# Alternating high and low products, with a short filler matmul, in the second part of each column tile of two input projections

## The chip, the cores and the metric

The kernel runs on one core of a Trainium2 chip. The metric is the device time of one execution in microseconds; the time of a kernel is the median of its runs.

## What is computed

The reference is a two-layer decoder trunk over 256 tokens of width 1024 in float32. Each layer is a half-step SwiGLU block (2816 hidden columns), a mixer, and a second half-step SwiGLU block. Layer 0 mixes with a short gated convolution, layer 1 with a sparse attention that reads keys and values made once between the layers. What the change touches is the second SwiGLU block of both layers:

```python
def swiglu_ffn(x, w_in, w_out):
    gate, up = jnp.split(x @ w_in, 2, axis=-1)
    return (jax.nn.silu(gate) * up) @ w_out
...
    h = h + 0.5 * swiglu_ffn(rmsnorm(h, ffn2_norm[i]), ffn2_w_in[i], ffn2_w_out[i])
```

Here `x @ w_in` is the input projection: 256 x 1024 by 1024 x 5632.

## The kernel before

**Split products.** Activations lie transposed, 128 features by 256 tokens in each of eight tiles. A float32 value is split into a high part, rounded to the operand type float32r, and a low part, the remainder in the same type. An activation tile `xs[k]` is 128 x 512: 256 columns of high parts, then 256 of low parts. A weight block of 128 x 128 has a high version `wh` (`u[0]`) and a low version `wl` (`u[1]`). One product of a block is then two matmuls: the *high product*, `wh` against all 512 columns of `xs[k]` (line 331), and the *low product*, `wl` against the 256 high columns (line 333). Both add into one PSUM bank; the two halves of the bank are added later. The next text calls one high and one low product a pair. Each matmul loads its own weights.

**Column tiles.** `ffn_in` makes an input projection. For each of 22 column tiles f it takes a double bank (`bank2`, tile `mm`, two of them in rotation) and fills two parts, the gate columns and the up columns, each by eight pairs (one for each k). `a_group` takes two weight units from the stream and calls `a_pass` for each part. `a_pass` issues the pairs in runs: `run` high products, then the `run` low products of the same k. `RUNS` sets a run of 2 for all tiles. In tile 0 both parts stop before k = 7, and a callback `mid` makes the row sums of the norm (`norm.rows`, which takes a bank from the pool `a` of four banks); after that come the last pairs. After a tile `total`, `times` and `ffn_evac` on ScalarE and VectorE make the hidden columns (lines 342 to 359).

**Weights.** `Stream` brings the weights by DMA from SyncE. Units of 128 x 1024 are split by ScalarE (high, line 150) and VectorE (low, line 167), up to `NBUF` = 6 units ahead. `weave` puts these conversions between the steps of an evacuation. A tile gives its two units back after its last matmul (`W.done`).

**Order.** The kernel is scheduled by hand: each engine runs its instructions in program order. The two projections that the change touches stand between two output projections (`out_proj`, lines 440 and 442, in runs of 2 too) or, in layer 1, behind the attention.

**Other places named below.** `b_full` (lines 550 to 552) and lines 821 to 823 are projections whose matmuls are all of 512 columns. Line 453 is a series of 256-column products at the end, line 656 one in the compression. Line 628 transposes 128 x 128 blocks; line 667 is two fp32 products of 64 columns; line 305 the fp32 product of the norm's row sums, 256 columns.

Of the kernel before, what the change touches and what calls it, by code (L numbers as in the profile page):

```python
# [9 lines left out]
F32 = mybir.dt.float32  # L10
# [6 lines left out]
P = 128  # L17
T = 256
# [15 lines left out]
LAG = 4  # L34
NBUF = 6
CHUNK = 2048
EXP4 = (0, 1, 2, 3, 4, 5)
ORDER = """
    q00.0 q00.1 q00.2 norm_pe q00.3 norm_act:A norm_dve:D q01.0 qsq00:A qsum00:D q01.1 uh6:A qsqrt00:A ul6:D q01.2 uh7:A qrec00:D ul7:D qrr00:P q01.3
# [22 lines left out]
def trunk(ctx, tc, A, out):  # L62
    nc = tc.nc
    ve, ac, pe, po, sy = nc.vector, nc.scalar, nc.tensor, nc.gpsimd, nc.sync
# [9 lines left out]
    def mk(shape, tag, bufs, dt=F32, pool=None):  # L74
        uid[0] += 1
        return (pool or sb).tile(list(shape), dt, tag=tag, name=f"{tag}_{uid[0]}", bufs=bufs)
# [4 lines left out]
    def bank(shape=(P, 512)):  # L81
        return mk(shape, "a", 4, pool=ps)

    def bank2():
        return mk([P, 2, 512], "mm", 2, pool=ps)
# [14 lines left out]
    class Stream:  # L100
# [7 lines left out]
        def add(self, src, lo=0, hi=None, joint=0):  # L108


            hi = src.shape[1] if hi is None else hi
            while lo < hi:
                n = min(CHUNK, hi - lo)
                for u in range(max(n // 1024, 1)):
                    self.where.append((len(self.src), u, joint))
                self.src.append(src[:, lo:lo + n])
                lo += n

        def load(self, c):
            while self.loaded <= min(c, len(self.src) - 1):  # L120
                st = mk([P, CHUNK], "ws", 3)
                src = self.src[self.loaded]
# [66 lines left out]
    W = Stream()  # L189
# [32 lines left out]
    h = [hall[:, c] for c in range(ND)]  # L222
    first = [mk([P, CHUNK], "ws", 3) for _ in range(2)]
    for q in range(6):
# [12 lines left out]
    ident = small[:, S_ID:S_ID + P]  # L237
# [6 lines left out]
    def tables():  # L244

        sy.dma_start(small, A["small"])
        po.memset(rb, NEG)
        sy.dma_start(rb[:NB], A["rel_bias"])
        oh = t2()
        sy.dma_start(oh[:NB + 1], A["onehot"])  # L250
        yield
        pr = bank()
        pe.matmul(pr[:16], rb, oh[:NB + 1], start=True, stop=True)
        row = t2()
        ac.activation(row[:16], pr[:16], AF.Copy, scale=-1.0)
        sy.dma_start(row_d, row[:16])


    def new_xs():
        return [mk([P, 512], "xs", 8, F32R) for _ in range(8)]  # L260
# [62 lines left out]

    RUNS = (2, 2, 2, 2)

    def a_pass(o, u, xs, ks, last=7, run=2):

        ks = list(ks)
        for i in range(0, len(ks), run):
            for k in ks[i:i + run]:  # L330
                pe.matmul(o, u[0][:, k * P:(k + 1) * P], xs[k], start=(k == 0), stop=False)  # L331
            for k in ks[i:i + run]:
                pe.matmul(o[:, :T], u[1][:, k * P:(k + 1) * P], xs[k][:, :T], start=False, stop=(k == last))  # L333
# [5 lines left out]
    def total(o, n):  # L339

        r = t2([P, n, T])
        ac.copy(r, o[:, :, T:])  # L342
        ve.tensor_tensor(out=r, in0=o[:, :, :T], in1=r, op=ALU.add)  # L343
        return r
# [4 lines left out]
    def weave(gen):  # L349
        for _ in gen:  # L350
            W.pump(1)
        W.pump()

    def ffn_evac(r, R, hid):
        times(r, R, 2)
        yield
        s = t1()
        ac.activation(s, r[:, 0], AF.Silu)  # L358
        ve.tensor_tensor(out=s, in0=s, in1=r[:, 1], op=ALU.mult)  # L359
        yield  # L360
        hd = act()
        split(s, hd)
        hid.append(hd)

    def a_group(parts, xs, mid=None, run=2):
        us = W.take(len(parts))
        if mid is None:
            for o, u in zip(parts, us):
                a_pass(o, u, xs, range(8), run=run)
        else:  # L370
            for o, u in zip(parts, us):
                a_pass(o, u, xs, range(7))
            mid()
            for o, u in zip(parts, us):
                a_pass(o, u, xs, [7])
        W.done(len(parts), False)

    def ffn_in(xs, norm, R=None, bg=None, pre=None, late=False):
        hid, sums = [], []
        box = [R]  # L380

        def mid():
            if pre is not None:
                pre()
            box[0] = norm.rows()

        for f in range(NF):
            o = bank2()
            if late and f < 2:

                u = W.take(2)
                a_pass(o[:, 0], u[0], xs, range(8))
                if f == 1:
                    W.pump(1)
                    mid()
                a_pass(o[:, 1], u[1], xs, range(8))
                W.done(2, False)
            else:
                a_group([o[:, 0], o[:, 1]], xs, mid if f == 0 and R is None else None, RUNS[f % 4])
            sums.append(total(o, 2))  # L400
            while len(sums) > (1 if late and f < LAG else 0):
                weave(ffn_evac(sums.pop(0), box[0], hid))
            if bg is not None:
                bg(f)
        return hid
# [57 lines left out]
    xs = new_xs()  # L463
    nm = Norm([(xs, G_FFN1)])
# [14 lines left out]
    half(1, 1)  # L479
    W.pump(2)  # L480
    hid = ffn_in(xs, nm, late=True)
    xs = new_xs()
    nm = Norm([(xs, G_MIX)])
# [39 lines left out]
    xs = new_xs()  # L523
    nm = Norm([(xs, G_FFN2)])
    tab = tables()
    next(tab)
    out_proj(zs, 1.0, nm)
    hid = ffn_in(xs, nm, pre=lambda: list(tab))


    xs = new_xs()
# [3 lines left out]
    nm = Norm([(xkv, G_KV), (xs, G_FFN1 + 8)])  # L535
# [172 lines left out]
    def bg(f):  # L708

        if f == 0:  # L710
            kv["s"] = squares(kns)
        elif f == 1:
            r = inv_rms(kv["s"])
            for tt in range(2):
                v = kns[tt].rearrange("p (n d) -> p n d", d=64)
                po.tensor_tensor(out=v, in0=v, in1=r[:, tt * 8:tt * 8 + 8, None].to_broadcast([P, 8, 64]), op=ALU.mult)
        elif f in (2, 3, 4, 5):
            c_trans((f - 2) % 2, (f - 2) // 2)
        elif f in (6, 7):
            k_trans(f - 6)  # L720
        elif f == 8:
            po.tensor_tensor(out=both, in0=ident[:, :64], in1=ident[:, 64:], op=ALU.add)
            po.tensor_tensor(out=both48, in0=ident[:96, :48], in1=ident[:96, 48:96], op=ALU.add)
        elif f == 9:
            kv["rk"] = rh_split(0)
        elif f == W1AT[0]:
            kv["ak"] = c_hidden(kv["rk"])
        elif f == 12:
            kv["ak"] = c_total(kv["ak"])
            kv["rv"] = rh_split(1)  # L730
            W.limit = NBUF
        elif f == W1AT[1]:
            kv["av"] = c_hidden(kv["rv"])
            kv["kc"] = kc_norm(c_second(kv["ak"], 0))
        elif f == 15:
            kv["av"] = c_total(kv["av"])
        elif f == 16:
            kc_trans(kv["kc"])
        elif f == 17:
            pc = c_second(kv["av"], 1)  # L740
            for q in range(4):
                ac.copy(vc[32 * q:32 * q + 15, q % 2].rearrange("p (b a d) -> p b a d", a=2, d=64)[:, :, q // 2],
                        pc[:15, :256].rearrange("p (b a d) -> p b a d", a=2, d=64)[:, :, q // 2])

    hid = ffn_in(xs, None, R1, bg)
    xs = new_xs()
    nm = Norm([(xs, G_MIX + 8)])
# [227 lines left out]
    def pair_ops(p):  # L975
# [138 lines left out]
        add(f"M0{p}", m0)  # L1114
        if p in EXP4:
            add(f"U0{p}", e0s)
# [115 lines left out]
    xs, nm = xs2, nm2  # L1232
    W.at = u0 + 9 + ND
    W.pump()
    del oT
    hid = ffn_in(xs, nm)
    class Store:
        def tile(self, c):
            sy.dma_start(out[c], h[c])
# [69 lines left out]
```

## Time and profile before

| | us |
|---|---|
| median of 3 runs | 988.7 |
| lowest, highest | 988.3, 990.07 |
| the profiled execution, its own time | 990.75 |
| span of the profiled execution | 988.9 |

The profile is of one execution. PE stands for TensorE's matmuls, PEld for its weight loads, DVE for VectorE, ACT for ScalarE, POOL for GpSimd, SP for SyncE; "mm<-xs,wl" means that the tile mm is written from xs and wl. In the timeline each row is a start in us, a duration, the engine and line, the operation, and how many such instructions follow each other; an instruction's end is modelled, and matmuls overlap in the records, so the distance of two starts is the cost of a step. In the rows of stretches, (x...) is the number of instructions, PEclk the granted share of TensorE's clock. The two projections in question run from about 288.0 to 412.2 us (layer 0) and from 801.0 to 924.0 us (layer 1); tiles 1 to 21 of them begin at 295.18 and 806.99 us.

### The profile page before, as it was taken

The numbers are of one execution on the slowest core, as the hardware profiler recorded it, in microseconds if no ns is written. First come the engines' busy times: TensorE is split into PE (matmuls) and PEld (weight loads), VectorE is DVE, ScalarE is ACT, GpSimd is POOL, SyncE is SP. The second block draws the span as 40 slices with busy tenths as digits, with TensorE's granted clock in tenths as the row PEclk, the third lists the DMA queues.
The fourth block names the chain that finished last, engine by engine and source line by source line (L and its number), as shares of the span: only waits on it lengthen the run. The fifth ranks groups of instructions, "written<-read, shape, count | busy, mean of one in ns | idle before, by whom it ended". The sixth has DMA issues, their size and how long they took to land.

```text
span 988.9 us, 14575 instructions
## 1 busy us (share of the span) xinstructions
PE 976.5 (99%) x5672; PEld 838.3 (85%) x5672; DVE 745.8 (75%) x1078; ACT 560.3 (57%) x905; POOL 163.8 (17%) x235
## 2 busy tenths in 40 slices
PE   8999999999999999999999999999989999999998
PEld 6888888888888888888888888888867788888887
DVE  7887876568888787867549988866589788787752
ACT  4765654445556565644556677644469466655530
POOL 5000001144460000011011022011256420000000
PEclk8999999999999999999999999999999999999999
DMA  7655555545546555565544566654810455655550
GB/s 236 240 207 176 206 203 181 179 151 197 205 141 245 176 204 174 198 204 195 174 140 155 203 223 213 209 203 149 229 71 1 133 173 206 199 185 187 202 186 22
DMA packets 28720, 177.58 MB, mean 180 GB/s; under 512 B 3259, under 2 KB 6587, under 8 KB 7916
## 3 DMA queue, kind: packets, MB, share of 16 engines
q1 hardware_dynamic: 28652, 176.66, 52.6%
q8 instruction: 44, 0.72, 0.3%
q14 instruction: 24, 0.20, 0.1%
HBM read 175.57 MB, written 1.08 MB: 179 GB/s over the span
## 4 chain that ended last, share of the span: by engine, by line
PE 96%; DVE 2%; POOL 1%; issue 0%; DMA 0%; ACT 0%; SPq 0%; POOLq 0%; DVEq 0%; ACTq 0%
PE mm L331 37%; PE mm L333 18%; PE a L440 17%; PE a L442 8%; PE a L331 3%; PE a L333 1%; PE a L550 1%; PE a L552 1%; PE a L551 1%; PE a L1065 1%; PE a L821 1%; PE mm L999 1%; PE a L1081 1%; PE a L822 1%; PE a L823 1%; PE mm L990 0%
## 5 line engine op out<-in xcount | busy, mean ns | idle before, releaser
L331 PE MATMUL mm<-xs,wh 128*128 128x512 f32 x1536 | 488.5, 399 | 2.7 <-DVE xs L281 2.2
L167 DVE TENSOR_TENSOR wl<-ws,wh 128x1024 fp32r<-128x1024 f32 x322 | 400.4, 1247 | 82.9 <-ACT wh L150 82.5
L150 ACT CAST wh<-ws 128x1024 fp32r<-128x1024 f32 x322 | 335.8, 1046 | 89.6 <-PE a L440 58.5
L333 PEld LDWEIGHTS mm<-xs,wl 128*128 128x128 f32 x1536 | 289.6, 189 | 69.1 <-DVE wl L470 0.8
L333 PE MATMUL mm<-xs,wl 128*128 128x256 f32 x1536 | 304.2, 279 | 0.5 <-DVE wl L470 0.5
L331 PEld LDWEIGHTS mm<-xs,wh 128*128 128x128 f32 x1536 | 235.8, 189 | 5.7 <-DVE xs L281 4.3
L440 PE MATMUL a<-act,wh 128*128 128x512 f32 x722 | 226.7, 395 | 0.0
L442 PEld LDWEIGHTS a<-act,wl 128*128 128x128 f32 x722 | 135.6, 188 | 32.1
L442 PE MATMUL a<-act,wl 128*128 128x256 f32 x722 | 141.8, 278 | 0.0
L343 DVE TENSOR_TENSOR t<-mm,t 128x512 f32<-128x512 f32 x96 | 66.1, 689 | 76.4 <-ACT t L342 75.7
L342 ACT COPY t<-mm 128x512 f32<-128x512 f32 x96 | 56.1, 585 | 103.6 <-PE mm L333 103.5
L440 PEld LDWEIGHTS a<-act,wh 128*128 128x128 f32 x722 | 109.9, 189 | 0.0
L358 ACT ACTIVATE t<-t 128x256 f32<-128x256 f32 x88 | 36.8, 419 | 63.7 <-DVE t L347 63.6
L347 DVE TENSOR_TENSOR t<-t,R 128x512 f32<-128x512 f32 x88 | 61.6, 700 | 2.8
L336 ACT CAST act<-t 128x256 fp32r<-128x256 f32 x96 | 39.0, 407 | 28.1 <-DVE t L504 19.1
L287 POOL TENSOR_TENSOR sq<-hall 128x256 f32<-128x256 f32 x5 | 3.1, 615 | 295.9 <-DVE hall L409 294.1
L290 POOL TENSOR_TENSOR t<-hall 128x256 f32<-128x256 f32 x35 | 27.4, 783 | 134.8 <-DVE hall L409 134.6
L280 ACT ACTIVATE xs<-hall,gains 128x256 fp32r<-128x256 f32 x40 | 19.7, 504 | 50.6 <-DVE hall L409 47.5
L337 DVE TENSOR_TENSOR act<-t,act 128x256 fp32r<-128x256 f32 x96 | 40.9, 426 | 4.3 <-ACT act L336 4.3
L409 DVE SCALAR_TENSOR_TENSOR hall<-a,hall 128x256 f32<-128x256 f32 x78 | 32.9, 422 | 14.4 <-PE a L442 12.1
L359 DVE TENSOR_TENSOR t<-t,t 128x256 f32<-128x256 f32 x88 | 36.9, 419 | 4.0 <-ACT t L358 4.0
L281 DVE SCALAR_TENSOR_TENSOR xs<-hall,gains,xs 128x256 fp32r<-128x256 f32 x40 | 27.5, 696 | 15.1 <-ACT xs L280 15.1
(238 smaller groups left out, 810.2 us busy)
## 6 DMA issues: line engine op xcount, KB each, us to landing
ws<-in_ffn_w_in_dram SPq DMA_DIRECT2D x86, 1024.0 KB, 4.9
ws<-in_ffn_w_out_dram SPq DMA_DIRECT2D x44, 1024.0 KB, 4.8
ws<-in_conv_w_in_dram SPq DMA_DIRECT2D x12, 1024.0 KB, 4.8
ws<-in_w_kv_dram SPq DMA_DIRECT2D x6, 1024.0 KB, 4.8
ws<-in_conv_w_out_dram SPq DMA_DIRECT2D x4, 1024.0 KB, 4.8
ws<-in_attn_w_q_dram SPq DMA_DIRECT2D x4, 1024.0 KB, 4.9
ws<-in_attn_w_o_dram SPq DMA_DIRECT2D x4, 1024.0 KB, 9.1
act<-row_d SPq DMA_DIRECT2D x8, 256.0 KB, 9.1
```

The costliest lines, as they stand in the source:

```text
L150: ac.copy(h, src)
L167: e.tensor_tensor(out=l, in0=src, in1=h.bitcast(F32), op=ALU.subtract)
L331: pe.matmul(o, u[0][:, k * P:(k + 1) * P], xs[k], start=(k == 0), stop=False)
L333: pe.matmul(o[:, :T], u[1][:, k * P:(k + 1) * P], xs[k][:, :T], start=False, stop=(k == last))
L336: ac.copy(dst[:, :T], src)
L337: ve.tensor_tensor(out=dst[:, T:], in0=src, in1=dst[:, :T].bitcast(F32), op=ALU.subtract)
L342: ac.copy(r, o[:, :, T:])
L343: ve.tensor_tensor(out=r, in0=o[:, :, :T], in1=r, op=ALU.add)
L347: ve.tensor_tensor(out=r, in0=r, in1=R[:, None, :].to_broadcast([P, n, T]), op=ALU.mult)
L359: ve.tensor_tensor(out=s, in0=s, in1=r[:, 1], op=ALU.mult)
L440: pe.matmul(o, wh, lhs[k], start=(k == 0), stop=False)
L442: pe.matmul(o[:, :T], wl, lhs[k][:, :T], start=False, stop=(k == n - 1))
```

## The change

`ffn_in` gets a table `mixed`, one entry (first, where, width) for each of the tiles 1 to 21. For these, the first part is issued by `a_pass` in runs of `first`. The second part goes through `a_mixed`, which alternates: one high product, one low product, for k = 0 to 7. Ahead of the high product of k = `where` stands one more matmul, the filler, if `width` isn't 0. With a positive width it multiplies the part's first high weight block with that many columns of `xs[0]`, in float32r; with a negative one it multiplies the fp32 identity with that many columns of `xs[0]` in fp32. It writes a bank of its own, `idle[0]`, which nobody reads and which comes from the pool `a` at the start of the projection.

The table for layer 0 has first = 8 throughout, fillers of 16, 32, 64, 96, 128, 192 and 256 columns, each ahead of k = 1, 2 and 3. The table for layer 1 has 21 mixed entries: three without a filler, eight of 64 columns, nine in fp32 (32, 64 and 128 columns) and one of 512 columns; first is 8 in ten of them, 4 in four, 2 in three and 1 in four.

```diff
+MIXED = (((8, 1, 16), (8, 2, 16), (8, 3, 16), (8, 1, 32), (8, 2, 32), (8, 3, 32), (8, 1, 64), (8, 2, 64), (8, 3, 64), (8, 1, 96), (8, 2, 96), (8, 3, 96), (8, 1, 128), (8, 2, 128), (8, 3, 128), (8, 1, 192), (8, 2, 192), (8, 3, 192), (8, 1, 256), (8, 2, 256), (8, 3, 256)),
+         ((2, 1, 0), (4, 1, 0), (2, 1, 64), (2, 2, 64), (4, 1, 64), (4, 2, 64), (4, 3, 64), (8, 1, -32), (8, 2, -32), (8, 3, -32), (8, 1, -64), (8, 2, -64), (8, 3, -64), (8, 1, -128), (8, 2, -128), (8, 3, -128), (1, 1, 0), (1, 1, 64), (1, 2, 64), (1, 3, 64), (8, 1, 512)))
...
+    def filler(width, u, xs):
+
+        if width < 0:
+            pe.matmul(idle[0][:, :-width], ident, xs[0][:, :-width].bitcast(F32), start=True, stop=True)
+        else:
+            pe.matmul(idle[0][:, :width], u[0][:, :P], xs[0][:, :width], start=True, stop=True)
+
+    def a_mixed(o, u, xs, where, width):
+
+        for k in range(8):
+            if k == where:
+                if width:
+                    filler(width, u, xs)
+            pe.matmul(o, u[0][:, k * P:(k + 1) * P], xs[k], start=(k == 0), stop=False)
+            pe.matmul(o[:, :T], u[1][:, k * P:(k + 1) * P], xs[k][:, :T], start=False, stop=(k == 7))
...
-    def ffn_in(xs, norm, R=None, bg=None, pre=None, late=False):
+    idle = [None]
+
+    def ffn_in(xs, norm, R=None, bg=None, pre=None, late=False, mixed=None):
+        if mixed is not None:
+            idle[0] = bank()
...
-                a_group([o[:, 0], o[:, 1]], xs, mid if f == 0 and R is None else None, RUNS[f % 4])
+                if mixed is None or f == 0:
+                    a_group([o[:, 0], o[:, 1]], xs, mid if f == 0 and R is None else None, RUNS[f % 4])
+                else:
+                    u = W.take(2)
+                    first, where, width = mixed[f - 1]
+                    a_pass(o[:, 0], u[0], xs, range(8), run=first)
+                    a_mixed(o[:, 1], u[1], xs, where, width)
+                    W.done(2, False)
...
-    hid = ffn_in(xs, nm, pre=lambda: list(tab))
+    hid = ffn_in(xs, nm, pre=lambda: list(tab), mixed=MIXED[0])
...
-    hid = ffn_in(xs, nm)
+    hid = ffn_in(xs, nm, mixed=MIXED[1])
```

## The prediction

> **What bounds the kernel now.** I read the page first: busy shares, the granted clock, the chain that ended last.
>
> ```profile
> span 988.9 us, 14575 instructions
> PE 976.5 (99%) x5672; PEld 838.3 (85%) x5672; DVE 745.8 (75%) x1078; ACT 560.3 (57%) x905; POOL 163.8 (17%) x235
> PEclk8999999999999999999999999999999999999999
> PE 96%; DVE 2%; POOL 1%; issue 0%; DMA 0%; ACT 0%; SPq 0%; POOLq 0%; DVEq 0%; ACTq 0%
> ```
>
> The chain runs through TensorE for 96% of the span, so what matters is what one matmul costs there. Busy shares don't tell that, because records of neighbouring matmuls overlap. I work with distances between starts. Then the two stretches that the change touches, column tiles 1 to 21 of each projection:
>
> ```profile
> core 0: us, PE busy (x) PEld busy (x) DVE busy (x) ACT busy (x) POOL busy (x), PEclk, DMA share, GB/s
> 295.18:412.22 117.04, 117.04 (x675) 102.12 (x674) 94.85 (x129) 70.32 (x106) 0.00 (x0) 1.00 0.58 198
> 806.99:924.03 117.04, 117.04 (x675) 102.12 (x674) 93.72 (x128) 70.48 (x106) 0.00 (x0) 1.00 0.58 196
> ```
>
> TensorE has no gap in either, and the clock is granted in full. VectorE needs 94.85 of 117.04 us and ScalarE 70.32. Both stretches take the same 117.04 us: 21 tiles of 5.573 us, two parts of eight pairs each, so a part is 2787 ns and a pair (one high product of 512 columns, one low of 256) is 348.3 ns. Whatever TensorE does more here lengthens the span by just that much. The timeline of TensorE shows the steady step, two high, two low:
>
> ```profile
> 380.17 0.63 PE L331 MATMUL mm<-xs,wh 128*128 128x512 f32 x2
> 380.64 0.39 PE L333 MATMUL mm<-xs,wl 128*128 128x256 f32 x2
> 380.87 0.63 PE L331 MATMUL mm<-xs,wh 128*128 128x512 f32 x2
> ...
> 399.68 0.63 PE L331 MATMUL mm<-xs,wh 128*128 128x512 f32 x2
> ```
>
> From 380.17 to 399.68 lie 28 steps of two pairs: 0.697 us each, 348.4 ns a pair. The high ones take 0.235, the low ones 0.115.
>
> **The change, part by part.** There are 42 tiles touched, each with a first part in a new run length and a second part that alternates; 39 of them get one filler. Everything else (weight units taken, where they are given back, evacuations) keeps its order.
>
> *Fillers.* A filler is a matmul with its own weight load, put ahead of a high product. How short can such a step be? These rows have the shortest steps with full 128x128 weights: four transposes of 128 columns, and two fp32 products of 64 columns, which the trace shows as four instructions.
>
> ```profile
> 524.38 0.60 PE L628 MATMUL a<-small,act 128*128 128x128 f32 x4
> L628 PE MATMUL a<-small,act x16: 272/272/273, 524.4 to 542.8; 128*128 128x128 f32 x16
> 584.55 0.40 PE L333 MATMUL mm<-xs,wl 128*128 128x256 f32 x2
> 584.78 0.56 PE L667 MATMUL a<-both,t 128*128 128x64 f32 x4
> 585.15 0.70 PE L331 MATMUL mm<-xs,wh 128*128 128x512 f32 x2
> 585.69 0.40 PE L333 MATMUL mm<-xs,wl 128*128 128x256 f32 x2
> ```
>
> Four transposes span 0.60 us, and one alone 0.272: (600-272)/3 = 109 ns from start to start. At L667 the low pairs stand 585.69-584.55 = 1.14 us apart instead of 0.697, so four passes of 64 columns cost 0.443 us, 111 ns each. The same floor for 64 and 128 columns, so it is the weight load, not the width. I take 111 ns for every single pass under 256 columns. For 256 columns and for fp32 at 256:
>
> ```profile
> 577.30 0.64 PE L656 MATMUL a<-wh,act 128*128 128x256 f32 x4
> ...
> 579.21 0.63 PE L331 MATMUL mm<-xs,wh 128*128 128x512 f32 x2
> 977.67 2.80 PE L453 MATMUL a<-act,wh 128*128 128x256 f32 x22
> 980.31 0.28 PE L456 MATMUL a<-act,wh 128*128 128x256 f32 x1
> 805.73 0.28 PE L333 MATMUL mm<-xs,wl 128*128 128x256 f32 x1
> 805.85 0.59 PE L305 MATMUL a<-sq,ones 128*128 128x256 f32 x2
> 806.09 0.58 PE L331 MATMUL mm<-xs,wh 128*128 128x512 f32 x1
> 806.51 0.28 PE L333 MATMUL mm<-xs,wl 128*128 128x256 f32 x1
> ```
>
> L656: 16 in 1.91 us, 119 ns each. L453: 22 in 2.64 us, 120 ns. L305 is one fp32 product of 256 columns as two passes: low to low 0.78 us instead of 0.35, so 0.43, or 0.216 a pass. Half the width would be 108 ns a pass, at the floor again. So an fp32 filler (widths 32, 64, 128) is two passes of 111 = 222 ns.
>
> First projection: 18 fillers of 16 to 192 columns at 111 = 1998 ns, three of 256 at 119 = 357. Second: eight of 64 columns at 111 = 888, nine in fp32 at 222 = 1998, one of 512 at 233 (the L550 rows below). Sum 5474 ns, **+5.5 us**. Bounds: 109 a pass below (5.4), 120 above (5.9). No other work hides it, as TensorE has no gap; a gain through the filler is a rival below.
>
> [...]
>
> *Alternation.* The trace holds a few stretches of one high, one low:
>
> ```profile
> 272.69 0.40 PE L331 MATMUL a<-act,wh 128*128 128x512 f32 x1
> ...
> 274.08 0.62 PE L440 MATMUL a<-act,wh 128*128 128x512 f32 x2
> 788.53 0.39 PE L331 MATMUL a<-act,wh 128*128 128x512 f32 x1
> ...
> 789.57 0.40 PE L331 MATMUL a<-act,wh 128*128 128x512 f32 x1
> 797.11 0.40 PE L331 MATMUL a<-act,wh 128*128 128x512 f32 x1
> ...
> 798.17 0.63 PE L331 MATMUL a<-act,wh 128*128 128x512 f32 x2
> ```
>
> Four pairs in 1.39 us and three in 1.04: 347.1 ns a pair on the mean. Three in 1.06 in the third: 353.3, a slower footing that short stretches fall into after other run lengths. I take 347.1, since two of three rows have it and a part lasts eight pairs: -1.3 ns for 336 pairs, **-0.4 us**. Bounds: 346.7 (-0.6 us) to 353.3 (+1.6).
>
> *First parts.* 31 of the 42 (all of the first projection, ten of the second) run eight high products and then eight low; four run four, four run one, three stay at two. Streams of high products stand in the shared key projection, on two footings:
>
> ```profile
> 473.52 0.39 PE L550 MATMUL a<-wh,pt 128*128 128x512 f32 x1
> ...
> 476.78 0.40 PE L552 MATMUL a<-wl,pt 128*128 128x512 f32 x1
> 701.70 0.39 PE L821 MATMUL a<-wh,xs 128*128 128x512 f32 x1
> ...
> 702.83 0.39 PE L823 MATMUL a<-wl,xs 128*128 128x512 f32 x1
> ```
>
> 14 steps in 3.26 us, 233 ns; and 5 in 1.13, 226. I take 233, which is nearest to the 0.235 of this very stage, and 119 for the low ones: 8 x 233 + 8 x 119 = 2816, 29 ns over 2787. Times 31: +0.9 us. Four runs of four, half of that: +0.06. Four runs of one: -0.04. Together **+0.9 us**; bounds 226 (-0.8) and 233 with 120 (+1.2).
>
> *At no cost.* The filler's bank comes out of the pool of four before the bank of the norm's row sums, so those sums get the bank of a later output column. TensorE meets that after seven of eight steps of tile 0, some 5 us on, and the sums need all output columns anyhow; without that cover it would be one evacuation, under a microsecond. Nobody reads the filler's bank, so no engine waits for it. DMA issues, VectorE and ScalarE instructions are the same; a part longer by 0.15 us gives them more room.
>
> **Sum.** 5.5 - 0.4 + 0.9 = +6.0 us. The profiled execution took 990.75 us for its span of 988.9; it would take 996.8. It stood 2.05 us over the median of the three runs, 988.7 (988.3 to 990.07), so for the median **994.7 us**. All lower bounds together give 988.7 + 5.4 - 0.6 - 0.8 = 992.7, all upper ones 988.7 + 5.9 + 1.6 + 1.2 = 997.4. A change of 0.2%, 2 us, is about what a measurement of this kernel can tell from none.
>
> **Rivals.**
> 1. *Narrow fillers are charged like fp32.* No row has a narrow product with the operand type of the main stream. For: the only narrow products (L667) appear as two passes. Against: the 256-column low products are single passes. Then the 26 narrow ones pay a second 111 ns, +2.9 us, and the three of 192 columns stream for 162 a pass instead of 111, +0.3: 997.9. If only the columns count fourfold and the load once, the 96, 128 and 192 wide cost +1.1: 995.8.
> 2. *The slow footing stays.* If each filler throws the alternation onto 353.3 and it doesn't come back: +2.1 us against my sum, 996.8. Against: the stretches in the trace that fell into it are short, and one at 272.69 is steady for all four pairs.
> 3. *A faster footing (faster than before).* [...] If it led into 226 + 110 = 336 ns a pair, and run lengths 8 kept it too: part two -11 x 336 = -3.7 us, the 31 long first parts (2688 instead of 2816) -4.0, the other eleven about -1. That is 986.0. It decides from about 337 ns a pair over all 672 pairs; in part two alone, 336 ns gives 991.0, still slower. Against: nothing in the trace pairs 226 with 110, and after every stall of the tiles above the step is 0.697 again. [...]
> 4. *It is hidden,* since VectorE's conversion of weights sets the pace: 94.85 of 117.04 us speak against it. 988.7.
>
> **How the numbers follow.** Forecast with its bounds 0.62 (own range 992.7 to 997.4); narrow as fp32 0.16; slow footing 0.08; a faster footing in part two alone 0.07 (about 991); the faster footing throughout 0.03; hidden 0.02; a cause not thought of 0.02. Slower takes all but the fast, the hidden and a small part of the 991 case: 0.92; faster 0.04, same 0.04. The range 991.8 to 998.2 leaves out the fast cases and the last tenths of the fp32 one.
>
> **What would show it.** Starts of TensorE in the stretches: 39 extra steps at 109 to 120 (fp32: two passes); eight low products in a row at 117 to 120; alternating pairs at 347; the two stretches together longer by 6 us, the first by some 2.8 (2.36 of fillers, 0.6 of long runs, -0.2), the second by 3.2; the other stages unchanged; no gap of TensorE. Wrong would be a filler under 100 ns, pairs that settle at another distance than 346 to 354, or two passes for the narrow ones.

## Result and the profile after

The changed kernel takes 995.86 us (median of 4 runs, 994.26 to 996.76) against 988.5 us before (988.14 to 990.07): 7.4 us more, ratio 1.0072 with a 95% interval of 1.0054 to 1.009. The forecast was 994.7 us in a range of 991.8 to 998.2, slower with a chance of 0.92.

The page of the changed kernel: busy shares, then the chain by engine.

```profile
span 993.2 us, 14671 instructions
PE 982.2 (99%) x5720; PEld 844.4 (85%) x5720; DVE 745.7 (75%) x1078; ACT 560.1 (56%) x905; POOL 164.5 (17%) x235
PE 95%; DVE 2%; POOL 1%; DMA 0%; issue 0%; ACT 0%; SPq 0%; POOLq 0%; DVEq 0%
```

TensorE has 48 matmuls more (39 fillers, of which nine are two instructions) and is still the chain. VectorE and ScalarE have the same numbers of instructions. The two stretches of tiles 1 to 21, and the output projection behind the first (columns: length, then busy time and count of each engine, granted clock, DMA):

```profile
293.99:414.12 120.13, 120.13 (x696) 105.33 (x695) 94.81 (x129) 70.32 (x106) 0.00 (x0) 1.00 0.57 193
807.41:928.25 120.84, 120.84 (x701) 105.92 (x700) 93.64 (x128) 70.44 (x106) 0.00 (x0) 1.00 0.55 190
414.12:475.42 61.30, 61.30 (x354) 53.49 (x353) 44.35 (x55) 30.79 (x40) 9.25 (x13) 1.00 0.57 193
```

They were 117.04 us each: +3.09 and +3.80, **+6.9 us** together, where 6.0 were forecast. TensorE has no gap in them. The output projection is at its 61.30 us, unchanged. The spans of the two profiles differ by 4.3 us only, since in two stages that the change leaves alone the profile of before was slower: from the first matmul of the first projection to its end, and the attention. Before:

```profile
6.18:137.06 130.88, 128.11 (x707) 109.53 (x708) 108.55 (x142) 78.83 (x120) 11.48 (x13) 0.97 0.61 210
701.01:800.97 99.96, 94.95 (x650) 72.38 (x649) 79.97 (x208) 69.01 (x188) 50.78 (x93) 0.98 0.36 113
```

After:

```profile
6.39:135.86 129.47, 127.78 (x706) 109.25 (x707) 107.83 (x142) 78.74 (x120) 12.15 (x13) 0.97 0.62 211
702.92:801.38 98.46, 93.47 (x651) 71.15 (x649) 80.48 (x208) 68.97 (x188) 50.68 (x93) 1.00 0.36 115
```

Neither belongs to the change: in the profiles of e1, e2, e3, e5 and e6 below, which run both stages with the same code, they take 129.8 to 130.1 and 98.5 to 99.9 us (the last section returns to the attention). From here on other stages than these two are compared; they agree to 0.02 us between kernels that run the same code in them.

Inside the stretches each step of TensorE can be read from the starts. In a tile of the first projection, (8, 1, 64), "x8" is the long run of eight high products that opens a first part:

```profile
328.26 2.03 PE L349 MATMUL mm<-xs,wh 128*128 128x512 f32 x8
...
331.43 0.19 PE L333 MATMUL a<-xs,wh 128*128 128x64 f32 x1
331.46 0.48 PE L341 MATMUL mm<-xs,wh 128*128 128x512 f32 x1
331.77 0.28 PE L342 MATMUL mm<-xs,wl 128*128 128x256 f32 x1
331.89 0.40 PE L341 MATMUL mm<-xs,wh 128*128 128x512 f32 x1
...
334.01 2.03 PE L349 MATMUL mm<-xs,wh 128*128 128x512 f32 x8
```

The filler is one instruction, L333. From 331.89 to 334.01 six pairs take 2.12 us: 353 ns a pair, until the tile ends. This is the slow footing (a footing is the steady pace that a stream settles on). In the neighbour (8, 2, 64), with the filler one pair later, the same distance gives another number:

```profile
337.54 0.19 PE L333 MATMUL a<-xs,wh 128*128 128x64 f32 x1
...
337.99 0.40 PE L341 MATMUL mm<-xs,wh 128*128 128x512 f32 x1
...
338.34 0.39 PE L341 MATMUL mm<-xs,wh 128*128 128x512 f32 x1
...
339.73 2.00 PE L349 MATMUL mm<-xs,wh 128*128 128x512 f32 x8
```

From 337.99 five pairs in 1.74 us, 348 ns, of which the first still settles; the last four, from 338.34, take 1.39: 347 ns, the fast footing. Over all tiles the first parts cost 0.4 us more than before and the second parts 6.5. The experiments part these into fillers, run lengths and alternation.

### The profile page after: what moved, and what is told of

The parts are those of the page before. It is cut to its first block, busy times and chain, and to the rows that moved or that the text cites. A ratio compares the mean times of both kernels' runs of the same rounds, so it can differ in the third digit from the quotient of the medians.

```text
span 993.2 us, 14671 instructions
## 1 busy us (share of the span) xinstructions
PE 982.2 (99%) x5720; PEld 844.4 (85%) x5720; DVE 745.7 (75%) x1078; ACT 560.1 (56%) x905; POOL 164.5 (17%) x235
## 4 chain that ended last, share of the span: by engine, by line
PE 95%; DVE 2%; POOL 1%; DMA 0%; issue 0%; ACT 0%; SPq 0%; POOLq 0%; DVEq 0%
PE mm L349 29%; PE a L469 17%; PE mm L351 14%; PE a L471 8%; PE mm L341 8%; PE mm L342 4%; PE a L349 3%; PE a L351 1%; PE a L579 1%; PE a L581 1%; PE a L580 1%; PE a L1094 1%; PE a L850 1%; PE mm L1028 1%; PE a L1110 1%; PE a L851 1%
## 5 line engine op out<-in xcount | busy, mean ns | idle before, releaser
L351 PEld LDWEIGHTS mm<-xs,wl 128*128 128x128 f32 x1200 | 212.3, 189 | 43.1 <-DVE wl L169 0.5
L351 PE MATMUL mm<-xs,wl 128*128 128x256 f32 x1200 | 225.5, 280 | 0.1
L349 PEld LDWEIGHTS mm<-xs,wh 128*128 128x128 f32 x1200 | 192.9, 189 | 16.6 <-DVE xs L283 3.6
L342 PE MATMUL mm<-xs,wl 128*128 128x256 f32 x336 | 94.2, 280 | 0.0
L341 PEld LDWEIGHTS mm<-xs,wh 128*128 128x128 f32 x336 | 63.3, 188 | 11.6
L342 PEld LDWEIGHTS mm<-xs,wl 128*128 128x128 f32 x336 | 63.6, 189 | 0.1
```

## Experiments

My theory after the result: the fillers cost what a weight load costs, some 5.8 us; the rest, 1 us more than a fast alternation would give, comes from a second, slower footing of the alternating stream, which lasts. The rivals: the alternation is slow by itself, or the fillers cost more than they show.

**Alternation alone** (e1): no filler, first parts in runs of two.

```diff
-MIXED = (((8, 1, 16), (8, 2, 16), ...
+MIXED = (((2, 1, 0),) * 21,) * 2
```

> No filler anywhere; all 42 tiles run their first part in runs of two and alternate in the second. Theory 'fillers cost, alternation settles by how it is entered': as in the one such tile of the changed kernel (2786 + 2773 ns, -14 against before), so the two stretches of 21 tiles together are 0.6 us shorter than before (233.5 instead of 234.08 us), total 988 us, no difference that can be measured. Rival 'alternation itself goes to the slow footing': 353.3 ns a pair, +1.7 us in the stretches, 990.3.

```profile
294.16:410.92 116.76, 116.76 (x675) 102.00 (x673) 94.82 (x129) 70.34 (x106) 0.00 (x0) 1.00 0.55 199
804.22:920.98 116.76, 116.76 (x675) 101.97 (x673) 93.66 (x128) 70.43 (x106) 0.00 (x0) 1.00 0.55 196
```

-0.28 us in each: all 42 second parts take 2773 or 2774 ns, 346.6 a pair. The total is 987.64 us, ratio 0.9994 (0.9984 to 1.0004), as expected no difference that can be measured. Alternation is not slow by itself.

**Fillers alone** (e2): runs of two everywhere, the same 39 fillers ahead of k = 2.

```diff
-        for k in range(8):
-            if k == where:
-                if width:
-                    filler(width, u, xs)
-            ...
+        for i in range(0, 8, 2):
+            if i == 2 and width:
+                filler(width, u, xs)
+            a_pass(o, u, xs, range(i, i + 2))
...
-                    a_pass(o[:, 0], u[0], xs, range(8), run=first)
+                    a_pass(o[:, 0], u[0], xs, range(8))
```

> The 39 fillers, all ahead of k = 2, in parts that keep runs of two; no alternation, no long runs. Theory 'a filler costs its weight load, about 111 to 120 ns a pass': stretches +5.5 us (239.6), 994. [...]

```profile
294.83:414.35 119.52, 119.52 (x696) 104.53 (x695) 94.84 (x129) 70.34 (x106) 0.00 (x0) 1.00 0.54 194
809.11:929.47 120.36, 120.36 (x702) 105.32 (x701) 93.71 (x128) 70.45 (x106) 0.00 (x0) 1.00 0.53 191
332.20 0.40 PE L349 MATMUL mm<-xs,wl 128*128 128x256 f32 x2
332.43 0.20 PE L333 MATMUL a<-xs,wh 128*128 128x64 f32 x1
332.46 0.71 PE L347 MATMUL mm<-xs,wh 128*128 128x512 f32 x2
333.01 0.39 PE L349 MATMUL mm<-xs,wl 128*128 128x256 f32 x2
...
852.17 0.31 PE L331 MATMUL a<-xs,small 128*128 128x32 f32 x2
```

+2.48 and +3.32, together **+5.8 us**; total 995.9 us, ratio 1.0074 (1.0061 to 1.0087). The total is 7.3 us over the kernel before, more than the stretches show, but its four executions had a mean granted clock of 0.993 or 0.994, and those of the kernel before at that clock took 989.9 to 991.2 us: against them it is some 5.4 us more. Around the 64-column filler the low products stand 0.81 us apart instead of 0.697: 113 ns. Every one of the 20 fillers of 16 to 96 columns lengthens its part by 113 ns, whatever its width; the six of 128 and 192 by 126, the three of 256 by 120, the one of 512 by 233. The fp32 ones are two instructions ("x2", 32 columns here) and cost 231 to 253. Up to 96 columns the width made no difference; that the filler's weight load sets this price fits, but no run has a filler without one. The narrow float32r filler is one instruction at 113 ns and not 222, so the rival "charged like fp32" is out.

**Runs of eight alone** (e3): second parts in runs of two as in e2, and

```diff
-MIXED = (((8, 1, 16), (8, 2, 16), ...
+MIXED = (((8, 1, 0),) * 21,) * 2
```

> All 42 first parts in a run of eight high and eight low products; second parts in runs of two; no fillers. By the prediction 2816 ns a part: +1.2 us (235.3 in the stretches). By the changed kernel's own tiles (mean 2796, between 2775 and 2816): +0.4 us. Either is near the edge of what the total can tell; the trace's stretches decide.

```profile
294.20:411.38 117.18, 117.18 (x674) 102.69 (x673) 94.77 (x129) 70.36 (x106) 0.00 (x0) 1.00 0.56 198
```

+0.14 us, and +0.13 in the second stretch: 2793 or 2794 ns a first part instead of 2787. Total 988.96 us, ratio 1.0006 (0.9997 to 1.0015).

**Alternation behind runs of eight** (e5): the same table, with second parts that alternate.

> All 42 first parts in a run of eight, second parts alternating, no filler. Theory 'the footing is set by how the alternation is entered, and a run of eight puts it on the slow one': every second part at 353.3 ns a pair, 2827 ns (+40), with +7 for the first part: stretches +2.0 us, total about 990.5. Rival 'the filler throws it off': without fillers the alternation is fast as after runs of two, 2773 ns (-14), stretches -0.3 us, 988.3.

```profile
294.42:412.17 117.75, 117.75 (x674) 103.25 (x673) 94.84 (x129) 70.30 (x106) 0.00 (x0) 1.00 0.55 197
```

+0.71 us, and +0.70 in the second stretch. All 42 second parts take 2831 to 2833 ns, 354 a pair: the slow footing from the first pair to the last, with no filler at all. (41 of the first parts, which follow a slow one, run in 2774 to 2776 ns, so the sum is below the 2.0 us expected.) The same alternating code differs by 58 ns a part, according to what stands ahead of it. The total, 991.9 us, ratio 1.0029 (1.0018 to 1.0041), is more than the 1.4 us of the stretches. The granted clock accounts for much of the rest: three of the seven executions had 0.996 or 0.997 and took 989.9 to 990.7 us, 1.4 to 2.1 us more than the 988.5 of the kernel before at 0.996 (mean of seven); the other four had 0.993 or 0.995 and took 991.9 to 992.4.

**The filler's place** (e6):

```diff
-MIXED = (((8, 1, 16), (8, 2, 16), ...
+MIXED = (((8, 2, 64),) * 21, ((8, 1, 64),) * 21)
```

> First parts in a run of eight and a filler of 64 columns in all 42 tiles: ahead of k = 2 in the first projection, ahead of k = 1 in the second. Theory 'the filler shifts the footing and the place decides': as in the changed kernel's own tiles with these entries, second parts of about 2908 ns throughout the first projection (fast after the filler) and 2930 throughout the second (slow), 0.5 us between the two stretches. Rival 'the place has no part in it, the footing wanders by chance': both stretches a mixture with the same mean.

```profile
294.16:413.86 119.70, 119.70 (x696) 105.22 (x695) 94.82 (x129) 70.28 (x106) 0.00 (x0) 1.00 0.54 194
807.15:927.79 120.64, 120.64 (x695) 105.39 (x694) 93.71 (x128) 70.47 (x106) 0.00 (x0) 1.00 0.53 190
```

In the first stretch all second parts are 2907 or 2908 ns, in the second all 2930 or 2931. No mixture: the place of the filler decides the footing behind it, tile after tile. That it is the place and not the projection, the changed kernel shows: in its first projection the tiles (8, 1, 64) and (8, 2, 64) take 2930 and 2908 ns, in its second (2, 1, 64) and (2, 2, 64) take 2931 and 2908. The stretches differ by 0.94 us and not 0.5, because the next first part feels it too (2792 and 2816 ns). Against e5, the same stream without a filler, a tile is 93 ns longer with the filler ahead of k = 2 and 138 ns longer with it ahead of k = 1: what a filler adds here is its own step, 113 ns in e2, and what it does to the footing behind it. The one execution took 994.5 us.

**Alternation everywhere** (e4), from the kernel before:

```diff
-    RUNS = (2, 2, 2, 2)
+    RUNS = (1, 1, 1, 1)
-    def a_pass(o, u, xs, ks, last=7, run=2):
+    def a_pass(o, u, xs, ks, last=7, run=1):
-    def a_group(parts, xs, mid=None, run=2):
+    def a_group(parts, xs, mid=None, run=1):
```

> The kernel before with runs of one in every projection and output projection (about 2360 pairs), no fillers. If alternation, once on its fast footing, stays there through undisturbed streams: 346.5 instead of 348.3 ns a pair, -4 us, 984.5, faster. If it falls to the slow footing of 353.3 at the first disturbance and stays there: up to +11 us, near 1000. A mixture would show stretches of both, each constant between two stalls.

The total goes from 986.18 to 997.64 us in 12 executions (median 991.72; ratio 1.0034, 1.0011 to 1.0057). In the profiled one, 986.18 us, the two stretches (116.48 us each) and the output projection between them are fast. The first stretch and that projection:

```profile
292.27:408.75 116.48, 116.48 (x674) 102.70 (x673) 94.87 (x129) 70.45 (x106) 0.00 (x0) 1.00 0.56 199
408.75:469.77 61.02, 61.02 (x354) 53.80 (x353) 44.26 (x55) 30.85 (x40) 9.28 (x13) 1.00 0.55 194
```

In the third input projection, where other matmuls stand between the tiles, some tiles are fast and some slow. Its last 64 pairs and the 176 of its output projection, 240 in a row, are all slow, 353 ns, and that output projection takes 62.19 us instead of 61.31. A footing lasted through 240 pairs in a row here.

**How is the footing chosen?** Six kernels without fillers vary the runs of two ahead of the alternation. e7 and e8 give each pass of eight (and each output column) one or two runs of two and then single pairs:

```diff
-    RUNS = (2, 2, 2, 2)
+    LEAD = 2        # e7; 4 in e8
+    def cuts(n):
+        at = list(range(0, min(LEAD, n), 2)) + list(range(LEAD, n))
+        return list(zip(at, at[1:] + [n]))
...
-        for i in range(0, len(ks), run):
-            for k in ks[i:i + run]:
+        for i, j in cuts(len(ks)):
+            for k in ks[i:j]:
...
-            for k0 in range(0, n, RUNS[c % 4]):
+            for k0, k1 in cuts(n):
```

> The kernel before with every pass of eight (and every column of the output projections) in one run of two and then alternating; no fillers. If one run of two sets the fast footing each time: about 1.8 ns for three quarters of some 2360 pairs, -3 us, 985.5, with the small spread of the kernel before. If one run of two isn't enough after a stall: stretches on the slow footing, a spread like the kernel that alternates throughout (986 to 998).

> As the last, with two runs of two ahead of the alternation. If the fast footing needs an undisturbed stream of runs of two ahead of it: fast nearly everywhere, about 1.8 ns for half of the pairs in passes of eight and most in the output projections, -2.5 us, 986, small spread. If the footing does not depend on the lead: no difference from one run of two.

```profile
295.60 0.63 PE L336 MATMUL mm<-xs,wh 128*128 128x512 f32 x2
...
298.38 0.62 PE L336 MATMUL mm<-xs,wh 128*128 128x512 f32 x2
...
301.19 0.40 PE L336 MATMUL mm<-xs,wh 128*128 128x512 f32 x1
```

With one run of two (e7, above) a part on the fast footing, 2777 ns by the unrounded starts, is followed by one on the slow, 2817, and so on through the stretch: 117.46 us. Its output projections, with one run of two in each column of 22 pairs, are slow throughout instead (62.00 us behind this stretch). Its total is 994.6 us, ratio 1.0059 (1.0046 to 1.0071). With two (e8) every part of both stretches is fast, 116.76 us; the total still is 992.15 us (1.0041, 1.0028 to 1.0054), since the first output projection and the convolution take 152.63 us together instead of 150.96, the third input projection 133.17 instead of 132.24 and its output projection 62.04 instead of 61.31. Stages that were entered on the slow footing stayed there. Both totals missed what I expected.

e9 alternates in the second part of every input projection and in every other output column; e10 alternates throughout, with runs of two only at the start of a stage.

```diff
-            for k0 in range(0, n, RUNS[c % 4]):
+            step = 2 if n == 8 or c % 2 == 0 else 1     # e9
+            step = 2 if n == 8 or c == 0 else 1         # e10
+            for k0 in range(0, n, step):
...
-                a_group([o[:, 0], o[:, 1]], xs, mid if f == 0 and R is None else None, RUNS[f % 4])
+                a_group([o[:, 0], o[:, 1]], xs, mid if f == 0 and R is None else None, (2, 1))     # e9
+                a_group([o[:, 0], o[:, 1]], xs, mid if f == 0 and R is None else None, (2, 1) if bg is not None or f < 6 else (1, 1))     # e10
```

The pair of numbers is the run length of the two parts; `bg` is set in the third input projection alone.

> No fillers. In all four input projections the first part keeps runs of two and the second alternates; in the output projections every other column alternates. Theory 'a part of four runs of two always leads to the fast footing': -14 ns for each of 88 parts and -40 for about 14 columns, 1.8 us less, 986.7. Rival 'output columns of 22 pairs fall on the slow footing as after short leads': up to +110 ns a column, no gain in total.

> No fillers. Alternation throughout, with a part or column of runs of two only at the start of each stage (in the third input projection, which has other matmuls between its tiles, at every tile). If a footing, once set, lasts until the next disturbance: 346.5 ns a pair in three input and three output projections, -2.6 us, 986, each of these stages at one constant step. If it is lost within undisturbed streams: steps of 353 appear in mid-stage, up to +4 us.

```profile
295.63:412.17 116.54, 116.54 (x674) 101.82 (x673) 94.91 (x129) 70.42 (x106) 0.00 (x0) 1.00 0.56 199
412.17:474.25 62.08, 62.08 (x355) 53.86 (x353) 44.29 (x55) 30.86 (x40) 9.26 (x13) 1.00 0.54 192
```

e10: the input projection is fast to its end, the output projection behind it slow to its end (+0.8 us); all four output projections of 22 pairs a column are slow. e9's input stretches are fast (116.76), its output projections between, 61.48; total 989.04 us, ratio 1.0003 (0.9992 to 1.0015), where 986.7 was expected. e10's total is 992.28 us (1.0035, 1.0021 to 1.0048), where 986 was expected. An output column has 22 pairs, eleven runs of two; a part of an input projection has four. So far one run and eleven had turned the fast footing, two and four had kept it. e11 and e12 test just this: ten runs of two at the start of the output projections, and three (e11) or four (e12) at the start of each of the first tiles of the input projections. In both the third input projection goes back to runs of two throughout.

```diff
+    def cuts(n, lead):
+        lead = min(lead, n)
+        at = list(range(0, lead, 2)) + list(range(lead, n))
+        return list(zip(at, at[1:] + [n]))
...
-            for k0 in range(0, n, RUNS[c % 4]):
+            for k0, k1 in cuts(n, n if n == 8 else 20 if c == 0 else 0):
...
-                a_group([o[:, 0], o[:, 1]], xs, mid if f == 0 and R is None else None, RUNS[f % 4])
+                a_group([o[:, 0], o[:, 1]], xs, mid if f == 0 and R is None else None, (99, 99) if bg is not None else (6, 0) if f < 6 else (0, 0))     # e11
+                a_group([o[:, 0], o[:, 1]], xs, mid if f == 0 and R is None else None, (99, 99) if bg is not None else (8, 0) if f < 6 else (0, 0))     # e12
```

Here the numbers are leads: how many pairs of a part come in runs of two before it alternates.

> As the last kernel, with two changes. In input projections 1, 2 and 4 the alternation of the tiles up to 5 is led in by three runs of two instead of four, and in the output projections by ten instead of eleven. Theory 'an even number of runs of two leads to the fast footing, an odd one to the slow': the input projections go to 353 ns a pair and stay there to the last tile (projection 2: about 126 us instead of 123.7), the output projections to the fast footing (61.0 us instead of 62.07). Rival 'the input projections are always fast and the output projections always slow, by their operands': no change in either.

> As the one before, with four runs of two in the lead of the input projections again, and runs of two throughout in the third. Theory 'even number': all three input and all output projections on the fast footing, 0.5 us less in each of the three (123.7 in projection 2) and 0.3 in each output projection, in all 2.3 us less than before, 986.3, faster by 0.2%. Rival 'operands': output projections 62.07, in all 0.5 us more than before or the same.

The first stretch of e11 and the output projection behind it (e12's take 116.54 and 61.05 us):

```profile
293.71:412.17 118.46, 118.46 (x674) 102.79 (x673) 94.86 (x129) 70.39 (x106) 0.00 (x0) 1.00 0.55 196
412.17:473.22 61.05, 61.05 (x354) 53.37 (x353) 44.30 (x55) 30.83 (x40) 9.27 (x13) 1.00 0.55 194
```

Three runs of two turn the footing: in e11 the second parts of tiles 1 to 5 are 2819, 2773, 2819, 2774 and 2820 ns, and as the last of them is slow the tiles from 6 on stay slow, 353 ns a pair to the end. Ten runs end on the fast footing: the output projections go from 62.08 to 61.05 us in both kernels. The rival "by the operands" is out. But ten is even, and in e11 the output projection shown comes behind a slow input projection: there an even number turned the footing (last section). e12, with even numbers everywhere, is the only kernel whose interval lies below 1, if barely: 987.68 us against 988.71, ratio 0.9987 (0.9976 to 0.9999), by the ratio 1.3 us less where 2.3 were expected. Its stages behind the first input projection, without the attention, sum to 2.0 us less than before. e11 takes 991.21 us (1.0019, 1.0005 to 1.0034).

## Why the prediction was right, and where it was off

The direction, the main cause and the size to 1.4 us were right: TensorE has no slack in the stretches, and each filler is a step on the path. That the total came so near is in part luck, since the first parts were put 0.5 us too high and the alternation 1.1 us too low. Term by term, in the stretches:

| | forecast, us | measured, us | from |
|---|---|---|---|
| fillers | +5.5 | +5.8 | e2 |
| first parts | +0.9 | +0.4 | starts of the changed kernel |
| alternation | -0.4 | +0.7 | remainder of 6.9 |
| sum | +6.0 | +6.9 | stretches |

The remainder takes the fillers at e2's price, though e6 shows that in an alternating stream a filler also moves the footing. The single changes add up all the same: 5.8 us of e2 and, for the 31 tiles with a run of eight, the 34 ns a tile of e5, 1.0 us, make 6.8 of the 6.9.

*Fillers.* 111 ns a pass, read from products of 64 columns, was 113 for up to 96 columns; 128 and 192 columns cost 126 and not 111, and an fp32 filler 231 to 253 and not 222. In e2 half of the extra at 128 and 192 columns lies in the step itself (354 ns from the filler to the second high product instead of 347) and half in the two low products behind it (235 ns instead of 228 or 229); why is not shown. In e2, in a stream of runs of two, no filler cost less than 113 ns.

*First parts.* I took 233 ns for each high product and 119 for each low one, 2816 ns a part. The 31 long first parts took 2775 to 2816 ns, according to the footing ahead of them, 2796 on the mean.

*Alternation.* This is the step that failed. I took 347.1 ns, "since two of three rows have it and a part lasts eight pairs", and held the third row, 353.3, for something that passes. The rows told of two lasting states: e11 holds the slow one and e10 the fast one through 264 pairs in a row, and e5 enters the slow one in all 42 parts. In the changed kernel the run of eight enters the slow footing, and the filler then turns some tiles to the fast one (347 ns a pair behind it in (8, 2, 64)) and leaves others (353 in (8, 1, 64)). The second rival was half right; its price for a slow stream throughout, 2.1 us over the forecast, is above the 1.1 us that the alternation took over its forecast.

*The rest.* A faster footing than some 346.5 ns a pair did not appear in any of the 12 kernels, so the third rival, with its 336 ns, is not borne out. That the filler's bank costs nothing held: tile 0, in which the norm's row sums take their bank, lasts 7.17 us before and after in the first projection and 6.02 and 6.03 us in the second, and the output projection behind the first is 61.30 us in both. Of the total of 7.4 us the stretches show 6.9; the difference lies inside the interval (5.3 to 8.9 us).

## What to carry to other kernels

A matmul with its own 128x128 weights cost about 113 ns here at 16 columns as at 96, and 120 at 256 (e2): the narrow ones were not cheap, and in stretches in which TensorE has no gap the 39 fillers added 5.8 us. The stream of matmuls of 512 and 256 columns ran on two steady paces here, 346.5 and 353.3 ns a pair, and what a short stretch of the trace showed lasted through 264 pairs in e10 and e11: look at how a pace was entered before taking it for a transient. Where such a stream can be entered in two ways, compare stages from start to start, to hundredths of a microsecond, rather than totals, and hold totals against each other only at the same granted clock (the kernel before took 987.7 to 988.1 us on the mean at 0.998 and 990.3 to 990.6 at 0.994).

## What the runs showed of the hardware that was not expected

**Two footings, and what goes with them.** The same alternating stream ran at 346.5 or 353.3 ns a pair, through 264 pairs in a row in e10 and e11. An even number of runs of two (2, 4, 10) kept the fast footing and an odd one (1, 3, 11) left it: in the profiles of e1 and e7 to e12, 362 of 366 entries from the fast footing go by this. From the slow footing the count alone doesn't decide: 40 of 257 entries go against it, the ten runs of e11 and the output columns of e7 among them.

The starts in the traces hold a closer sign. A stream of runs of two alternates between two patterns: in one the two low products take 116 and 112 ns (their row reads 0.39 us), in the other 113 and 119 (0.40 us). In each stretch of the kernel before, 168 runs alternate without a break, so an even number of runs ends on the same pattern. Over the profiles of before, after, e1, e3, e4 and e7 to e12, all 377 alternating streams (of four pairs or more) behind the first pattern are fast and all 275 behind the second slow; 19 behind neither went both ways. The tenth and last run of two in e11's output projection, and the tenth and eleventh in e10's:

```profile
418.91 0.39 PE L445 MATMUL a<-act,wl 128*128 128x256 f32 x2
419.14 0.40 PE L443 MATMUL a<-act,wh 128*128 128x512 f32 x1
```

```profile
418.91 0.39 PE L443 MATMUL a<-act,wl 128*128 128x256 f32 x2
419.14 0.63 PE L441 MATMUL a<-act,wh 128*128 128x512 f32 x2
419.60 0.40 PE L443 MATMUL a<-act,wl 128*128 128x256 f32 x2
419.83 0.40 PE L441 MATMUL a<-act,wh 128*128 128x512 f32 x1
```

What follows is fast in e11 and slow in e10. This is a regularity found afterwards; no run set the pattern by other means, so that it is the cause is not shown. A run of eight led to the slow footing (e5, 354 ns a pair), and a filler turned it or left it by its place (e6, second parts of 2908 or 2930 ns). Why there are two footings is not shown by any run.

**The clock after a pause of TensorE.** In the attention TensorE waits 2.4 us for VectorE, in every profile. In the profile of before the granted clock is a half for 3.41 us around the end of that wait; in the profile of after it stays full:

```profile
735.24:738.65 3.41, 3.12 (x14) 2.71 (x16) 1.59 (x4) 1.09 (x3) 3.00 (x4) 0.50 0.00 0
735.53 1.09 PE L894 MATMUL a<-small,t 128*128 128x128 f32 x4 [2.41 <-DVE sm L1046]
```

```profile
734.90:739.90 5.00, 2.54 (x19) 1.77 (x18) 4.12 (x9) 2.20 (x4) 3.31 (x5) 1.00 0.00 0
737.44 0.63 PE L923 MATMUL a<-small,t 128*128 128x128 f32 x4 [2.40 <-DVE sm L1075]
```

The same pause, but four transposes of 1.09 against 0.63 us, and an attention of 99.96 against 98.46 us. All 14 profiles go by this: nine have no half clock there, and the stage takes 98.5 to 98.7 us; in before, e2 and e12 the half clock lasts 3.41 us and the stage 99.8 to 100.0; in e10 it comes twice for 3.41 us, the second time 41 us on, and in e11 once for 6.83, and the stage takes 101.2 to 101.4. So the half clock came in five of 14 profiles, for 3.41 us or twice that, though the pause of 2.4 us is in all of them. Why in these five is not shown. The totals of the kernel before follow its granted clock as well: in the rounds of the experiments its executions took 987.7 to 988.1 us on the mean at 0.998, 988.4 to 988.6 at 0.996 and 990.3 to 990.6 at 0.994.
